# An encoder layer with mLSTM and attention: softmax sums over 64 rows, a second exp, dm in four steps, updates ahead of kw

## The chip, the cores and the metric

The kernel runs on one core of one Trainium2 chip. The core has a matrix engine (TensorE, "PE" in the profile, with its weight loads as "PEld"), a vector engine (VectorE, DVE), a scalar engine for activations (ScalarE, ACT), GpSimd (POOL) and SyncE (SP), which issues DMAs. Each engine executes its own instructions in the order in which they stand in its queue; semaphores make one wait for another. DMAs are issued from the queues of SP, ACT and POOL. The metric is the device time of one execution in microseconds (us), the median of several runs.

## What is computed

One encoder layer, run over 2048 prompt tokens and 256 sample tokens with the same weights, all in float32, width 1024:

```
h = rmsnorm(x, norm1_w)
mq, mk, mv, mo, gates, aq, ak, av = split(h @ w_in)
m_out = sigmoid(mo) * norm(mlstm_forward + mlstm_backward)     # 8 heads of 64
a_out = softmax(rope(aq) rope(ak)^T / 8) av                    # 8 query heads, 2 key heads of 64
x = x + concat(m_out, a_out) @ w_out
a, g = split(conv3(rmsnorm(x, norm2_w) @ w_up))
x = x + (silu(g) * a) @ w_down                                 # then a final rmsnorm
```

Attention is over the whole segment: queries of the prompt see the 2048 prompt tokens, queries of the sample the 256 sample tokens. mLSTM is a gated linear recurrence, computed in tiles of 128 tokens: inside a tile the products of queries and keys are multiplied by decay factors exp(dm), and between tiles a state C is carried on.

## The kernel before

Stages. `phase_a` (to about 250 us of the profile) computes the attention projections and the gates. Then `run_both` interleaves two generators, `attention` and `mlstm`, by costs that each yields, and when `mlstm` is done (about 1440 us) it calls on `phase_c`, the output projection, in its place. Attention ends at about 1840 us, `phase_c` at about 1915 us, and the rest is the feed-forward part, `phase_d`. Most float32 products are made of three fast matmuls of split operands: a value x is kept as a high part `hi` (a rounded copy) and a low part `lo = x - hi`, and x*y becomes hi*hi + hi*lo + lo*hi.

The program's order is not the final one. A scheduler takes the instructions as the code issues them, with priorities (`tc.high_priority`), and lays them out on each engine by a simulated time; after that the order on each engine is fixed, and only semaphores delay it. A tile of a pool with `bufs=n` can be written again when the one n before it has had its last reader.

Attention works on blocks of 512 queries (`hbs`): 32 large ones (4 query tiles of one head, 16 key tiles) and 4 small ones (2 key tiles). For block n:

- `prep` loads and transposes the queries, `maxstep` (L548) makes one 128x512 piece of scores `px` and its row maximum `mx` on DVE; a block needs 16, which are done during the steps of the block before.
- `scores(kp)` (L568) makes two key tiles' scores `ps` in PSUM, by two matmuls each (L575, L576), the second of which also subtracts the maximum. ACT exponentiates in place (L579) and copies to `ph` (L580), and DVE makes `pl = ps - ph` (L581). `px`, `ps` and other short-lived results share four PSUM banks (`SCB = 4`, tag "sc").
- `values(kp)` (L585) adds six matmuls into the single PSUM bank `pv` (L594), three for each key tile: vh*ph, vl*ph, vh*pl. `vh` has 66 columns: 64 of V and two of ones, so row 64 of `pv` is the sum of the probabilities. `values` runs `PLAG = 3` steps behind `scores`, with 8 buffers each of `ph` and `pl`; the last three steps of a block are done at its end.
- `fin1` (L596) copies 65 rows of `pv` to `o1` on ACT and sends row 64 to DRAM (`rs_d`), from where it is read back as `rc`, 128x4. `fin2`, in step 3 of the next block, takes the reciprocal on DVE (L609), writes it to DRAM and reads it back as `rb`, broadcast to 64 rows. `fin3`, in step 5, multiplies on POOL (L616) and writes the result to `mix_d`. `phase_c` reads `mix_d` as `cmx`.

mLSTM works on four pairs of heads. `proj_steps` (L891) goes through blocks of 256 tokens: `proj` (L714, L747 for the last pair) makes keys, queries, values and output gates; `projT` (L776) transposes the keys of the block before on PE into `mt`, copies them on ACT to `mkt` (L783, one buffer), and POOL multiplies them by weights into `kw` (L787, two buffers, one for each tile of 128); `upd` (L791) makes the state updates `mu` from `kw` (L800) and copies them to `C`, two steps behind `proj`. In one step `projT(b - 1)` is issued ahead of `upd(2b - 4)` and `upd(2b - 3)`.

`out_steps` (L907) makes a pair's outputs, tile by tile, beside the next pair's projections:

- `out_l` (L814) loads `dm`, 128x512, by a broadcast DMA from POOL's queue (L818), one tile ahead; `DMB = 4` buffers.
- `out_a` (L822) masks both directions on POOL (L825, affine_select), exponentiates the four parts on ACT (L828) and, for the first three pairs, loads the output gates `og` from POOL's queue (L833).
- `out_b`, one step on, multiplies `dm` by the scores `mS` on DVE (L844) and takes the part of the carried state, `mI`; `out_c`, two steps on, makes `mN` from `dm` and the values (L859) and divides by the denominator (L862 to L865); `rstd_of` makes `mr` on POOL; `out_n`, three steps on, applies it (L876); `out_d`, six steps on, transposes and writes to `mix_d`.

`proj_steps` and `out_steps` issue `projT`, `upd`, `out_b`, `out_c`, `out_n` and `out_d` at high priority.

Of the kernel before, what the change touches and what calls it, by code (L numbers as in the profile page):

```python
# [57 lines left out]
QZB = 2  # L58
RWM = 4
S1B = 2  # L60
DMB = 4
KWB = 2
CSTEP = 1
LEAD = 1.3
# [3 lines left out]
RW = 4  # L68
PO = 4
PB = 4  # L70
PHB = 8
PLB = 8
PLAG = 3
ZT = 3
SG = 3
RS = 2
# [384 lines left out]
def attention(g, tc, s1, s2, pp):  # L461
# [12 lines left out]
    def load_kv(grp, k0, k1, after=None):  # L474

        if (grp, k0) in kv:
            return
        n = k1 - k0
        sp = s2 if n == NT1 else s1
        kv[(grp, k0)] = parts = []  # L480
        for t0 in range(0, n, 4):
            m = min(4, n - t0)
            s = f"{n}_{t0}"
            kk = sp.tile([P, m * P], F32R, tag="kk" + s, name=f"kk{grp}_{s}", bufs=1)
            kl1 = sp.tile([65, m * P], F32R, tag="kl1" + s, name=f"kl1{grp}_{s}", bufs=1)
            vs = [sp.tile([P, m, HD + 2 * (1 - a)], F32R, tag=f"v{a}" + s, name=f"v{a}{grp}_{s}", bufs=1)
                  for a in range(2)]
            c = slice((k0 + t0) * P, (k0 + t0 + m) * P)
            if after is not None:
                for t in (kk[0:1, 0:1], kk[HD:HD + 1, 0:1], kl1[0:1, 0:1], vs[0][0:1, 0, 0:1], vs[1][0:1, 0, 0:1]):  # L490
                    nc.gpsimd.tensor_copy(t, after[0:1, 0:1])
            nc.gpsimd.memset(f32(vs[0][:, :, HD:]), 1.0)
            for r in (0, HD):
                nc.gpsimd.dma_start(f32(kk[r:r + HD, :]), g.k_d[grp, 0:HD, c])
            nc.gpsimd.dma_start(f32(kl1[0:HD, :]), g.k_d[grp, HD:P, c])
            nc.gpsimd.memset(f32(kl1[64:65, :]), 1.0)
            for a in range(2):
                nc.gpsimd.dma_start(f32(vs[a][:, :, 0:HD]), g.v_d[a, grp, :, k0 + t0:k0 + t0 + m])
            parts.append((kk, kl1, vs))
# [68 lines left out]
    def scores(s, kp):  # L568
        N = s.N
        parts = []  # L570
        for z in range(2):
            ps = pp.tile([P, 512], F32, tag="sc", name=f"ps{s.nm}_{kp}_{z}")[:, 0:N]
            kk, kl1, _ = s.kv[kp // 2]
            kc = (2 * kp + z) % 4 * P
            nc.tensor.matmul(ps, kk[:, kc:kc + P], s.qq[:, 0:N], start=True, stop=False)  # L575
            nc.tensor.matmul(ps, kl1[:, kc:kc + P], s.qm[:, 0:N], start=False, stop=True)  # L576
            ph, pl = (sp.tile([P, 512], F32R, tag=t, name=f"{t}{s.nm}_{kp}_{z}", bufs=n)[:, 0:N]
                      for t, n in (("ph", PHB), ("pl", PLB)))
            nc.scalar.activation(ps, ps, AF.Exp)  # L579
            nc.scalar.activation(ph, ps, AF.Copy)  # L580
            nc.vector.tensor_tensor(pl, ps, f32(ph), ALU.subtract)  # L581
            parts.append((ph, pl))
        return kp, parts

    def values(s, kp, parts):  # L585

        N = s.N
        if kp == 0:
            s.pv = pp.tile([P, 512], F32, tag="pv", name="pv" + s.nm, bufs=1)
        for z, (ph, pl) in enumerate(parts):  # L590
            kt = 2 * kp + z
            vh, vl = (v[:, kt % 4, :] for v in s.kv[kp // 2][2])
            for k, (v, p) in enumerate(((vh, ph), (vl, ph), (vh, pl))):
                nc.tensor.matmul(s.pv[0:HD if k == 1 else HD + 2, 0:N], v, p, start=(kt == 0 and k == 0), stop=(kt == s.nk - 1 and k == 2))  # L594

    def fin1(s):  # L596

        N = s.N
        s.o1 = sp.tile([HD + 1, 512], F32, tag="o1", name="o1" + s.nm, bufs=2)
        nc.scalar.activation(s.o1[:, 0:N], s.pv[0:HD + 1, 0:N], AF.Copy)  # L600
        s.n = len(done)
        done.append(s)
        nc.scalar.dma_start(g.rs_d[s.n:s.n + 1, 0], s.o1[HD:HD + 1, :])
        s.rc = sp.tile([P, 4], F32, tag="rc", name="rc" + s.nm, bufs=2)
        nc.sync.dma_start(s.rc, g.rs_d[s.n, 0].rearrange("(p k) -> p k", k=4))

    def fin2(s):

        nc.vector.reciprocal(s.rc, s.rc)  # L609
        nc.sync.dma_start(g.rs_d[s.n, 1].rearrange("(p k) -> p k", k=4), s.rc)  # L610
        s.rb = sp.tile([HD, 512], F32, tag="rb", name="rb" + s.nm, bufs=1)
        nc.sync.dma_start(s.rb, g.rs_d[s.n:s.n + 1, 1].to_broadcast([HD, 512]))

    def fin3(s):
        N = s.N
        nc.gpsimd.tensor_tensor(s.o1[0:HD, 0:N], s.o1[0:HD, 0:N], s.rb[:, 0:N], ALU.mult)  # L616
        for t0, (h, q0, q1) in part(s):
            r0 = HD * (h % 2)
            nc.gpsimd.dma_start(g.mix_d[q0 // 2:q1 // 2, r0:r0 + HD, 4 + h // 2].rearrange("n p t -> p n t"),
                                s.o1[0:HD, t0 * P:(t0 + q1 - q0) * P].rearrange("p (n t) -> p n t", t=BT))  # L620

    def fin4(s):

# [1 line left out]
            if h == 7:  # L625
                g.mixed.update(range(q0, q1))

    done = []
    cur = prep(0)
    while cur.todo:  # L630
        maxstep(cur)
# [4 lines left out]
    for n in range(len(hbs)):  # L636
# [3 lines left out]
        for kp in range(nkp):  # L640
# [11 lines left out]
                if not nxt.todo:  # L652
                    prep2(nxt)
            if old is not None:
                if kp == min(3, nkp - 1):
                    fin2(old)
                if kp == min(5, nkp - 1):
                    fin3(old)
# [10 lines left out]
                maxstep(nxt)  # L669
            prep2(nxt)  # L670
        old, cur = cur, nxt
    fin2(old)
    fin3(old)
    fin4(old)

# [1 line left out]
def mlstm(g, tc, s1, sp, sw, sn, pj_, pm):  # L677
# [141 lines left out]
                            g.nm_d[i, 4 * s.p:4 * s.p + 4].rearrange("r l -> (r l)").unsqueeze(0).to_broadcast([P, 4 * P]))  # L819
        return o  # L820

    def out_a(s, i, o):  # L822
        for d in range(2):
            sgn = 1 - 2 * d
            nc.gpsimd.affine_select(out=o.dm[:, d], in_=o.dm[:, d], compare_op=ALU.is_ge, fill=NEG, base=0,  # L825
                                    pattern=[[0, 2], [sgn, P]], channel_multiplier=-sgn)
            for h in range(2):
                nc.scalar.activation(o.dm[:, d, h], o.dm[:, d, h], AF.Exp,  # L828
                                     bias=tm[:, i, 0, d, 2 * s.p + h:2 * s.p + h + 1])
        if s.p < LASTP:  # L830
            if i % 2 == 0:
                s.og = s1.tile([P, 2, P], F32, tag="ogT", name=f"ogr{s.p}_{i}", bufs=OTB)
                nc.gpsimd.dma_start(s.og, g.og_d[s.p, i // 2])  # L833
            o.og = s.og[:, i % 2]

    def out_b(s, i, o):
        nm = f"{s.p}_{i}"
# [479 lines left out]
def body(tc, aps, phases="abcd"):  # L1317
# [5 lines left out]
    with ExitStack() as st:  # L1323
# [13 lines left out]
        dram("q_d", [NT, P, 8, P])  # L1337
        dram("k_d", [2, P, T])
        dram("v_d", [2, 2, P, NT, HD])
        dram("rs_d", [36, 2, 512])  # L1340
# [167 lines left out]
```

## Time and profile before

| What | us |
|---|---|
| median of 3 runs | 3524.24 (3521.58 to 3526.81) |
| the profiled execution's own time | 3521.41 |
| its span, first to last instruction | 3519.7 |
| window 0 to 250 (`phase_a`): PE busy | 215.02 |
| window 1840 to 1915 (end of `phase_c`): PE busy | 68.07 |
| window 1915 to 3520 (`phase_d`): PE busy | 1556.60 |

The profile's rows are read so. A group of instructions: line, engine, operation, what it writes and reads, shapes, count; then busy us in total and mean ns of one; then the idle time of the engine just before them and what ended most of it. A wait: who waited, for whom, us in total, times, the longest. A row of the timeline: start, duration, engine, line, operation, and in brackets the idle time of the engine before it with the instruction that ended it. Windows are in us from the start of the span. The matmuls of PE overlap, so the busy time of PE is that in which at least one was under way; the ends are modelled.

### The profile page before, as it was taken

To read this page: it belongs to the slowest core of one execution; us is meant where nothing else is said; L and a number is where in the kernel's file an instruction comes from. 1 tells how busy PE (TensorE), PEld (TensorE's weight loads), DVE (VectorE), ACT (ScalarE), POOL (GpSimd) and SP (SyncE) were. 2 spreads that over 40 slices of the span, in tenths; PEclk is the share of its full clock that TensorE was granted. 3 is DMA by queue.
4 is the path that set the end of the run, shared out by engine and by line. 5 is a ranking of instruction groups with operands and counts; after the bars stand their busy time and mean duration, and the time that the engine had idled before them with its cause. 6 is when DMAs were issued, how large, how long until landed. Compare 5 with 4: busy or idle time off the path is not lost. (4 is left out here: it accounts for less than half of the span.)

```text
span 3519.7 us, 56010 instructions
## 1 busy us (share of the span) xinstructions
PE 3362.7 (96%) x20058; PEld 3065.6 (87%) x20058; DVE 2562.9 (73%) x4546; ACT 1922.3 (55%) x4293; POOL 1109.7 (32%) x1312
## 2 busy tenths in 40 slices
PE   7989999999999999899989999999999999999998
PEld 6788887788888778687758999999999999999998
DVE  6874566566657676766654887878887879877777
ACT  4445656665666666545552544445544445655555
POOL 6653032223215322111115333224433224422222
PEclk9999999999999999999989999999999999999999
DMA  6765433243346445432228333213423223322221
GB/s 219 242 204 155 123 94 112 83 131 109 98 130 184 129 131 146 127 105 86 67 61 265 119 98 102 72 66 123 139 95 107 70 69 123 132 66 73 72 67 55
DMA packets 271310, 409.24 MB, mean 116 GB/s; under 512 B 44020, under 2 KB 168724, under 8 KB 271032
## 3 DMA queue, kind: packets, MB, share of 16 engines
q1 hardware_dynamic: 243312, 363.11, 32.4%
q0 software_dynamic: 11088, 33.04, 3.7%
q10 hardware_dynamic: 16632, 9.52, 0.9%
q8 instruction: 158, 2.59, 0.3%
q14 instruction: 120, 0.98, 0.1%
HBM read 321.52 MB, written 84.05 MB: 115 GB/s over the span
## 5 line engine op out<-in xcount | busy, mean ns | idle before, releaser
L1247 PE MATMUL pd<-act,wd 128*128 128x384 f32 (+1 forms) x3120 | 594.2, 337 | 23.1 <-DVE acc L1249 12.5
L1247 PEld LDWEIGHTS pd<-act,wd 128*128 128x128 f32 x3120 | 541.2, 189 | 30.6 <-DVE acc L1249 16.6
L581 DVE TENSOR_TENSOR pl<-ps,ph 128x512 fp32r<-128x512 f32 x520 | 351.3, 687 | 251.4 <-ACT ph L580 247.2
L1109 PE MATMUL pa<-nt,wut 128*128 128x386 f32 (+2 forms) x2376 | 453.7, 339 | 4.5 <-ACT u L1125 4.5
L1109 PEld LDWEIGHTS pa<-nt,wut 128*128 128x128 f32 x2376 | 420.6, 189 | 5.1 <-ACT u L1125 5.1
L553 DVE TENSOR_REDUCE mx<-px 128x1 f32<-128x512 f32 (+1 forms) x528 | 347.5, 676 | 69.7 <-PE px L552 67.2
L579 ACT ACTIVATE ps<-ps 128x512 f32<-128x512 f32 x520 | 297.5, 586 | 176.7 <-PE ps L576 165.8
L594 PE MATMUL pv<-ph,v 128*66 128x512 f32 (+1 forms) x1040 | 340.0, 404 | 24.6 <-ACT ph L580 24.1
L1203 DVE SCALAR_TENSOR_TENSOR y<-u,cw,y 128x768 f32<-128x768 f32 (+1 forms) x264 | 314.3, 1191 | 36.9 <-ACT y L1196 29.9
L1114 POOL TENSOR_TENSOR tw<-ru 128x512 f32<-128x512 f32 x66 | 93.4, 1416 | 739.7 <-DMA ru<-w_up 643.0
L1249 DVE TENSOR_TENSOR acc<-pd,acc 128x384 f32<-128x384 f32 (+1 forms) x544 | 281.2, 538 | 33.8 <-PE pd L1247 32.7
L1125 ACT ACTIVATE u<-pa 128x386 f32<-128x386 f32 (+2 forms) x264 | 128.4, 486 | 324.7 <-PE pa L1109 322.8
L580 ACT ACTIVATE ph<-ps 128x512 fp32r<-128x512 f32 x520 | 300.8, 597 | 7.8
L993 PEld LDWEIGHTS po<-cmx,wo 128*128 128x128 f32 x1728 | 231.5, 192 | 32.0 <-ACT cmx L979 11.3
L993 PE MATMUL po<-cmx,wo 128*128 128x256 f32 x1728 | 241.1, 284 | 12.2 <-ACT cmx L979 10.2
L575 PE MATMUL ps<-qq,kk 128*128 128x512 f32 x520 | 217.4, 421 | 2.9 <-ACT qm L566 1.7
L552 PE MATMUL px<-kk,qq 128*128 128x512 f32 (+1 forms) x528 | 212.8, 417 | 6.0 <-DVE mx L553 5.0
L594 PEld LDWEIGHTS pv<-ph,v 128*66 128x66 f32 (+1 forms) x1040 | 136.0, 138 | 85.8 <-ACT ph L580 35.1
L594 PE MATMUL pv<-pl,v 128*66 128x512 f32 x520 | 210.2, 404 | 0.3
L576 PE MATMUL ps<-qm,kl 65*128 65x512 f32 x520 | 207.6, 402 | 0.2 <-ACT qm L566 0.2
L721 PEld LDWEIGHTS mj<-mn,wm 128*128 128x128 f32 x1296 | 187.3, 196 | 23.2 <-DMA mn<-n_d 3.4
L721 PE MATMUL mj<-mn,wm 128*128 128x256 f32 x1296 | 201.2, 291 | 5.1 <-DMA mn<-n_d 3.2
(287 smaller groups left out, 7144.6 us busy)
## 6 DMA issues: line engine op xcount, KB each, us to landing
ru<-w_up SPq DMA_DIRECT2D x132, 512.0 KB
mn<-n_d SPq DMA_DIRECT2D x216, 256.0 KB
rd<-w_down SPq DMA_DIRECT2D x66, 512.0 KB
n_d<-n1T SPq DMA_DIRECT2D x18, 1024.0 KB
dm<-nm_d POOLq DMA_DIRECT2D x72, 256.0 KB, 3.9
mjn<-n_d SPq DMA_DIRECT2D x72, 256.0 KB
mvn<-n_d SPq DMA_DIRECT2D x72, 256.0 KB
q_d<-qz SPq DMA_DIRECT2D x18, 512.0 KB
```

What stands on the lines that cost most here:

```text
L553: nc.vector.tensor_reduce(s.mx[:, t, z0:z0 + 1], ps[:, 0:w], AX.X, ALU.max)
L575: nc.tensor.matmul(ps, kk[:, kc:kc + P], s.qq[:, 0:N], start=True, stop=False)
L579: nc.scalar.activation(ps, ps, AF.Exp)
L580: nc.scalar.activation(ph, ps, AF.Copy)
L581: nc.vector.tensor_tensor(pl, ps, f32(ph), ALU.subtract)
L594: nc.tensor.matmul(s.pv[0:HD if k == 1 else HD + 2, 0:N], v, p, start=(kt == 0 and k == 0), stop=(kt == s.nk - 1 and k == 2))
L721: nc.tensor.matmul(pj[:, o], s.w[c][:, a, o * P:(o + 1) * P], nT[c][:, :, h, :], start=(c + o + k == 0), stop=(c == NCC - 1 and k == 2 and ...
L993: nc.tensor.matmul(po[:, o], wo[c][z // 2][:, a, n], mx[c][:, h, :], start=(c == 0 and k == 0), stop=(c == NCC - 1 and k == 2))
L1109: nc.tensor.matmul(p, w[:, aa, c, :], ops[k][:, c, bb, 0:n], start=c == 0 and i == 0 and not add, stop=c == NCC // 2 - 1 and i == 2, skip_ ...
L1203: nc.vector.scalar_tensor_tensor(y[:, s:e], u[:, s + k:e + k], cw[:, k, jj:jj + 1], y[:, s:e], ALU.mult, ALU.add)
L1247: nc.tensor.matmul(po, wds[j][c // 4][:, aa, c % 4 * P:(c % 4 + 1) * P], acts[j][:, bb, z0:z1], start=(j == 0 and k == 0), stop=(j == len( ...
L1249: nc.vector.tensor_tensor(accs[c][:, z0:z1], po, accs[c][:, z0:z1], ALU.add)
```

## The change

- `ph` is written by a first exp from `ps`; a second exp then writes `ps` in place. The copy goes.
- The high part of V gets 128 columns, 64 of V and 64 of ones, so that rows 64 to 127 of `pv` each hold the sums. `values` does the four matmuls with `ph` first and then the two with `pl`. `PLAG` goes from 3 to 2, and `ph` and `pl` from 8 buffers to 6.
- `fin1` copies the 64 rows of sums to `rs` on ACT and no longer goes through DRAM; `fin2` takes the reciprocal of 64x128 in place, and is called four times, once in each of the first four steps of the next block (or four times in the last step of a short one); `fin3` multiplies by `rs`. Three DMAs a block and the tiles `rc`, `rb` and `rs_d` go.
- `out_a` is divided: `out_m` masks and loads the gates, `out_a` holds the exps and comes one step later; `out_b`, `out_c` and `out_n` come one step later too; `out_l` for the next tile is issued behind the mask. `dm` gets 6 buffers. `out_a` is now at high priority.
- In `proj_steps`, `upd` comes ahead of `projT`: `projT(b - 1)` goes behind the first yield.

```diff
-DMB = 4
+DMB = 6
-PHB = 8
-PLB = 8
-PLAG = 3
+PHB = 6
+PLB = 6
+PLAG = 2
...
-            vs = [sp.tile([P, m, HD + 2 * (1 - a)], F32R, tag=f"v{a}" + s, name=f"v{a}{grp}_{s}", bufs=1)
+            vs = [sp.tile([P, m, P if a == 0 else HD], F32R, tag=f"v{a}" + s, name=f"v{a}{grp}_{s}", bufs=1)
...
+            nc.scalar.activation(ph, ps, AF.Exp)
             nc.scalar.activation(ps, ps, AF.Exp)
-            nc.scalar.activation(ph, ps, AF.Copy)
             nc.vector.tensor_tensor(pl, ps, f32(ph), ALU.subtract)
...
-        for z, (ph, pl) in enumerate(parts):
-            kt = 2 * kp + z
-            vh, vl = (v[:, kt % 4, :] for v in s.kv[kp // 2][2])
-            for k, (v, p) in enumerate(((vh, ph), (vl, ph), (vh, pl))):
-                nc.tensor.matmul(s.pv[0:HD if k == 1 else HD + 2, 0:N], v, p, start=(kt == 0 and k == 0), stop=(kt == s.nk - 1 and k == 2))
+        vs = [[v[:, (2 * kp + z) % 4, :] for v in s.kv[kp // 2][2]] for z in range(2)]
+        todo = [(vs[z][k], parts[z][0]) for z in range(2) for k in range(2)] + [(vs[z][0], parts[z][1]) for z in range(2)]
+        for k, (v, p) in enumerate(todo):
+            nc.tensor.matmul(s.pv[0:HD if k in (1, 3) else P, 0:N], v, p, start=(kp == 0 and k == 0),
+                             stop=(2 * kp + 2 == s.nk and k == 5))
...
-        s.o1 = sp.tile([HD + 1, 512], F32, tag="o1", name="o1" + s.nm, bufs=2)
-        nc.scalar.activation(s.o1[:, 0:N], s.pv[0:HD + 1, 0:N], AF.Copy)
...
-        nc.scalar.dma_start(g.rs_d[s.n:s.n + 1, 0], s.o1[HD:HD + 1, :])
-        s.rc = sp.tile([P, 4], F32, tag="rc", name="rc" + s.nm, bufs=2)
-        nc.sync.dma_start(s.rc, g.rs_d[s.n, 0].rearrange("(p k) -> p k", k=4))
+        s.o1 = sp.tile([HD, 512], F32, tag="o1", name="o1" + s.nm, bufs=2)
+        s.rs = sp.tile([HD, 512], F32, tag="rs", name="rs" + s.nm, bufs=1)
+        nc.scalar.activation(s.o1[:, 0:N], s.pv[0:HD, 0:N], AF.Copy)
+        nc.scalar.activation(s.rs[:, 0:N], s.pv[HD:P, 0:N], AF.Copy)
+        s.left = list(range(0, N, P))
 
     def fin2(s):
 
-        nc.vector.reciprocal(s.rc, s.rc)
-        nc.sync.dma_start(g.rs_d[s.n, 1].rearrange("(p k) -> p k", k=4), s.rc)
-        s.rb = sp.tile([HD, 512], F32, tag="rb", name="rb" + s.nm, bufs=1)
-        nc.sync.dma_start(s.rb, g.rs_d[s.n:s.n + 1, 1].to_broadcast([HD, 512]))
+        if s.left:
+            r = s.rs[:, s.left[0]:s.left[0] + P]
+            s.left.pop(0)
+            nc.vector.reciprocal(r, r)
...
-                if kp == min(3, nkp - 1):
+                for _ in range(1 if kp < nkp - 1 else 4):
                     fin2(old)
...
-    def out_a(s, i, o):
+    def out_m(s, i, o):
+
         for d in range(2):
             sgn = 1 - 2 * d
             nc.gpsimd.affine_select(out=o.dm[:, d], in_=o.dm[:, d], compare_op=ALU.is_ge, fill=NEG, base=0,
                                     pattern=[[0, 2], [sgn, P]], channel_multiplier=-sgn)
-            for h in range(2):
-                nc.scalar.activation(o.dm[:, d, h], o.dm[:, d, h], AF.Exp,
-                                     bias=tm[:, i, 0, d, 2 * s.p + h:2 * s.p + h + 1])
...
+    def out_a(s, i, o):
+        for d in range(2):
+            for h in range(2):
+                nc.scalar.activation(o.dm[:, d, h], o.dm[:, d, h], AF.Exp,
+                                     bias=tm[:, i, 0, d, 2 * s.p + h:2 * s.p + h + 1])
...
-            if 1 <= b <= NB:
-                with tc.high_priority(offset=MPRI):
-                    projT(s, b - 1)
-            yield (6 if s.p < LASTP else 3) if b < NB else 0.5
             if 2 <= b:
                 with tc.high_priority(offset=MPRI):
                     upd(s, 2 * b - 4)
                     upd(s, 2 * b - 3)
+            yield (6 if s.p < LASTP else 3) if b < NB else 0.5
+            if 1 <= b <= NB:
+                with tc.high_priority(offset=MPRI):
+                    projT(s, b - 1)
             yield (6 if s.p < LASTP else 3) if b < NB else 0.5
...
-            if 2 <= i < NT + 2:
-                with tc.high_priority(offset=MPRI):
-                    out_c(s, i - 2, os_[i - 2])
-            if 1 <= i < NT + 1:
-                with tc.high_priority(offset=MPRI):
-                    out_b(s, i - 1, os_[i - 1])
-            if 3 <= i < NT + 3:
-                with tc.high_priority(offset=MPRI):
-                    out_n(s, i - 3, os_[i - 3])
-            for k in (i, i + 1) if i == 0 else (i + 1,):
-                if k < NT:
-                    os_[k] = out_l(s, k)
+            for lag, f in ((3, out_c), (2, out_b), (4, out_n), (1, out_a)):
+                if lag <= i < NT + lag:
+                    with tc.high_priority(offset=MPRI):
+                        f(s, i - lag, os_[i - lag])
+            if i == 0:
+                os_[i] = out_l(s, i)
             if i < NT:
-                out_a(s, i, os_[i])
+                out_m(s, i, os_[i])
+            if i + 1 < NT:
+                os_[i + 1] = out_l(s, i + 1)
```

More of the change, by code (lines that the diff above doesn't have):

```diff
@@ L589, in values @@
             s.pv = pp.tile([P, 512], F32, tag="pv", name="pv" + s.nm, bufs=1)
[L590 to L594 removed]
+        vs = [[v[:, (2 * kp + z) % 4, :] for v in s.kv[kp // 2][2]] for z in range(2)]
[3 more added lines that the diff above has]
+                             stop=(2 * kp + 2 == s.nk and k == 5))
     def fin1(s):
         N = s.N
[L599 to L605 removed]
+        s.o1 = sp.tile([HD, 512], F32, tag="o1", name="o1" + s.nm, bufs=2)
[3 more added lines that the diff above has]
+        s.left = list(range(0, N, P))
     def fin2(s):
[L609 to L612 removed]
+        if s.left:
+            r = s.rs[:, s.left[0]:s.left[0] + P]
+            s.left.pop(0)
+            nc.vector.reciprocal(r, r)
     def fin3(s):
         N = s.N
[L616 removed]
+        nc.gpsimd.tensor_tensor(s.o1[:, 0:N], s.o1[:, 0:N], s.rs[:, 0:N], ALU.mult)
         for t0, (h, q0, q1) in part(s):
@@ L619, in fin3 @@
             nc.gpsimd.dma_start(g.mix_d[q0 // 2:q1 // 2, r0:r0 + HD, 4 + h // 2].rearrange("n p t -> p n t"),
-                                s.o1[0:HD, t0 * P:(t0 + q1 - q0) * P].rearrange("p (n t) -> p n t", t=BT))
+                                s.o1[:, t0 * P:(t0 + q1 - q0) * P].rearrange("p (n t) -> p n t", t=BT))
     def fin4(s):
@@ L626, in fin4 @@
                 g.mixed.update(range(q0, q1))
-    done = []
     cur = prep(0)
@@ L671, in attention @@
         old, cur = cur, nxt
-    fin2(old)
+    for _ in range(4):
+        fin2(old)
     fin3(old)
@@ L1339, in body @@
         dram("v_d", [2, 2, P, NT, HD])
-        dram("rs_d", [36, 2, 512])
         dram("nm_d", [NT, 16, P])
```

## The prediction

> **What bounds the kernel now.** The page and the busy times by stage come first.
>
> ```profile
> span 3519.7 us, 56010 instructions
> PE 3362.7 (96%) x20058; PEld 3065.6 (87%) x20058; DVE 2562.9 (73%) x4546; ACT 1922.3 (55%) x4293; POOL 1109.7 (32%) x1312
> ...
> 250.00:1440.00 1190.00, 1141.87 (x7193) 962.51 (x7192) 763.38 (x1827) 735.66 (x2008) 326.98 (x680) 0.99 0.43 124
> 1440.00:1840.00 400.00, 381.15 (x2225) 304.20 (x2223) 258.47 (x468) 226.27 (x438) 51.37 (x49) 0.98 0.31 93
> ```
>
> After the window and its length the columns are PE, PEld, DVE, ACT, POOL busy, granted clock, DMA share, GB/s. The two windows are attention beside mLSTM, and attention beside the output projection; the edit touches nothing else but a short end behind them. PE is busy in 1141.87 of 1190 us and 381.15 of 400: it is the bound, and 48 + 19 = 67 us of idling are most of what can be won. What ends that idling is in the waits of PE's weight loads, for the first window and then the second, and behind them in those of ACT, POOL and DVE (first window; total, times, longest):
>
> ```profile
> PEld pv L594 <- ACT ph L580: 26.1, 20, 3.2
> PEld mN L859 <- ACT mkt L783: 6.2, 2, 5.1
> PEld ps L575 <- DVE pl L581: 5.8, 13, 0.5
> PEld px L552 <- DVE mx L553: 4.8, 12, 0.6
> ...
> PEld pv L594 <- ACT ph L580: 9.1, 13, 2.0
> PEld px L552 <- DVE mx L553: 9.0, 17, 2.6
> PEld ps L575 <- DVE pl L581: 4.4, 11, 0.5
> ...
> ACT dm L828 <- POOL dm L825: 155.5, 55, 10.9
> ...
> POOL dm L825 <- DMA dm<-nm_d: 186.4, 63, 4.8
> POOL kw L787 <- PE mu L800: 148.8, 35, 20.2
> POOL o L616 <- DMA rb<-rs_d: 133.6, 16, 26.3
> POOL dm L818 <- PE mN L859: 91.2, 21, 17.6
> ...
> DVE pl L581 <- ACT ph L580: 168.3, 143, 5.1
> DVE hh L876 <- POOL mr L98: 75.4, 43, 6.3
> ```
>
> The largest item is pv waiting for ph, 26.1 + 9.1 = 35.2 us in 33 waits. ph is late because ACT is: it executes in order and stood 155.5 us for the mask that POOL puts on dm. POOL in turn stood for kw, rb and dm's buffer. One such chain, from the timelines of POOL, ACT and PE:
>
> ```profile
> 547.78 1.19 POOL L787 TENSOR_TENSOR kw<-mkt,tm 128x256 f32<-128x256 f32 x2 [3.15 <-PE mu L800]
> 553.94 1.32 POOL L616 TENSOR_TENSOR o<-o,rb 64x512 f32<-64x512 f32 x1 [4.98 <-DMA rb<-rs_d]
> ...
> 556.21 0.59 POOL L818 DMA_DIRECT2D dm<-nm_d x1
> 560.17 0.77 POOL L825 TENSOR_SCALAR_AFFINE_SELECT dm<-dm 128x256 f32<-128x256 f32 x2 [3.36 <-DMA dm<-nm_d]
> 560.60 0.40 ACT L828 ACTIVATE dm<-dm,tm 128x128 f32<-128x128 f32 x1 [3.70 <-POOL dm L825]
> 560.91 0.58 ACT L580 ACTIVATE ph<-ps 128x512 fp32r<-128x512 f32 x1
> 561.54 0.68 PE L594 MATMUL pv<-ph,v 128*66 128x512 f32 x2 [1.12 <-ACT ph L580]
> ```
>
> POOL waits for rb until 553.94, issues the load of dm only at 556.21, masks at 560.17; ACT's exp of dm stands 3.70 us for it with a ph copy queued behind, and PE loses 1.12 us.
>
> **Two exps.** ACT's work stays the same, exp and copy taking as long:
>
> ```profile
> L580 ACT ACTIVATE ph<-ps 128x512 fp32r<-128x512 f32 x520 | 300.8, 597 | 7.8
> L579 ACT ACTIVATE ps<-ps 128x512 f32<-128x512 f32 x520 | 297.5, 586 | 176.7 <-PE ps L576 165.8
> ```
>
> An exp into SBUF is not in the trace; I take the copy's 597 ns. ph leaves ACT one operation sooner, 0.59 us. Over the 33 waits that is 19 us, as an upper figure, since some are shorter than 0.59. pl comes no sooner, and its matmuls now stand last in each group, behind four that need ph alone. **-19 us**.
>
> **Mask, buffers, kw, and no trip through DRAM.** The mask of a tile goes one step ahead of its exp, so ACT comes to a masked dm; six buffers let dm be loaded before the matmul two steps back has freed one (the 91.2 us row). The updates free the two kw buffers before kw asks for them (the 148.8 us row). fin3's product follows DVE instead of two DMAs (the 133.6 us row), and three DMAs a block leave the ACT and SP queues. Of the 35.2 us there remain 16 after the 19; I take two thirds, **-10 us**, since the other ACT waits are for PE's own scores. mN waiting for mkt is the kw chain (mkt's single buffer is held by kw): **-6 us**. The clock of 0.99 over 1190 us is 12 us lost to half-rate stretches behind idling; half of it, **-6 us**. At the end of attention
>
> ```profile
> 1843.34 0.59 ACT L600 ACTIVATE o<-pv 65x512 f32<-65x512 f32 x1 [7.13 <-DMA mix_d<-o]
> ...
> 1846.02 1.25 PE L993 MATMUL po<-cmx,wo 128*128 128x256 f32 x4 [7.42 <-ACT cmx L979]
> ```
>
> PE stands 7.42 us behind the rb trips of the last small blocks; **-4 us**. In all -45 us.
>
> Moving kw behind the updates has its own price: mt, mkt and kw now come half a projection step before the updates that use kw, not one and a half. If POOL is late, mu stands on PE with everything behind it; with POOL 27% busy (326.98 of 1190) I take **+1**, bound 0 to 0.63 us (kw's length, half of the 1.19 above) for each of 36 = 23.
>
> **The reciprocal** is the price. 36 of 128x4 go, 144 of 64x128 come. Rows near it (min/median/max ns):
>
> ```profile
> L864 DVE RECIPROCAL dn<-dn x72: 147/178/181, 445.0 to 1433.5; 128x4 f32<-128x4 f32 x72
> L862 DVE SCALAR_TENSOR_TENSOR dn<-s x72: 148/158/1177, 444.6 to 1432.8; 128x4 f32<-128x4 f32 x72
> L131 DVE TENSOR_SCALAR rcol_a<-rs_a x18: 143/150/159, 9.1 to 189.6; 128x1 f32<-128x1 f32 x18
> L876 DVE TENSOR_TENSOR hh<-hh,mr 128x128 f32<-128x128 f32 x72 | 21.9, 304 | 78.6 <-POOL mr L98 75.4 <-ACT ps L579 2.9
> ```
>
> At an element a step like L876 a piece costs 0.30 us, 44 in all. Were all of the 178 ns due to its 4 elements, 5.7 us and 820 in all. But it takes 20 ns more than L862 of equal size and 28 more than the TENSOR_SCALAR, 5 to 7 ns an element; with the 1.2 ns an element between L862 and L876 (146 ns over 124) that is 158 + 124 x 6.2 = 0.93 us to 150 + 124 x 8.2 = 1.17. I take their middle, 1.05 us: 151 us of DVE, less 6 for the old ones. DVE's share of the two windows goes from 1022 of 1590 us (64%) to 73%. The Trainium skill (VectorE: DVE Perf Modes, First, the fixed hardware budget) states that a reciprocal iterates its divide with a repeat count of 8; by its 0.96 GHz (Specifications) I estimate 1.07 us beside the fixed part, some 175 us for all. The excess in the rows points the same way as the page, not to the 0.30.
>
> This stretches DVE's queue, not PE's directly. PE's waits for DVE above are 5.8 + 4.8 + 9.0 + 4.4 = 24 us; each stands for one of four score banks. I let them nearly double, **+20 us**. What keeps it there: DVE itself stood 168.3 us for ph and 75.4 for POOL's mr, and both shrink with the stalls above. Bounds: 0, and the rival below.
>
> **Smaller costs.** Copying the sums takes 36 x 0.59 = 21 us of ACT, which has 454 us free in the first window; 0, at worst 21 as the single pv bank is held longer. The V weights grow from 66 to 128 columns in 1040 matmuls:
>
> ```profile
> L594 PEld LDWEIGHTS pv<-pl,v 128*66 128x66 f32 x520 | 72.5, 139 | 25.1 <-DVE pl L581 5.2 <-issue 0.4
> L552 PEld LDWEIGHTS px<-kk,qq 128*128 128x128 f32 x528 | 100.2, 192 | 28.9 <-DVE mx L553 13.8 <-DVE pl L581 2.7 <-issue 0.5
> ...
> 1526.54 0.39 PE L575 MATMUL ps<-qq,kk 128*128 128x512 f32 x1
> 1526.77 0.39 PE L576 MATMUL ps<-qm,kl 65*128 65x512 f32 x1
> 1527.00 0.39 PE L594 MATMUL pv<-pl,v 128*66 128x512 f32 x1
> ```
>
> A load of 128 columns takes 53 ns more, yet L576 behind it starts 0.23 us after its forerunner just as L594 behind 66 columns does: hidden, **+2**. The lag of values behind scores falls from three steps to two, so at a block's end 6 matmuls instead of 12 (0.23 us each) cover the last ph; scheduled fillers take part of it, 0 here, and a rival.
>
> **Sum.** -45 + 1 + 20 + 2 = -22 us. The profiled execution took 3521.4 us (its span and 1.7 around), so 3499.4; the median of the runs is 2.8 above it: **3502**.
>
> **Rivals.**
> 1. All the waits go. 35.2 + 6.2 + 7.4 of waits and the 12 of clock, less 9 of costs: -52, 3472. For it: one cause, ACT and POOL in order, is behind them all. Against: PE's waits for DVE cannot fall with more DVE work.
> 2. The short lag eats the gain. 1.38 us less cover a block, 0.59 regained by the early ph: 0.79 x 36 = 28 more, +6, 3530. For it: each block ends with scores whose ph is used at once. Against: 260 steps (the 520 copies of ph, two each) in 1590 us are 6.1 us each, so two still give 12 us in mid-block.
> 3. DVE becomes the bound, slower. The four pieces fall into a block's first four steps, where the next block's 16 maxima stand too. Two such halves:
>
> ```profile
> 646.90:673.00 26.10, 23.92 (x158) 20.60 (x158) 17.18 (x34) 12.80 (x38) 6.04 (x13) 1.00 0.32 99
> 1504.00:1529.00 25.00, 25.00 (x174) 22.32 (x173) 17.69 (x34) 9.50 (x19) 5.24 (x5) 1.00 0.46 133
> ```
>
> DVE is busy 17.18 and 17.69 us there, so 8.1 us on average are free, and 4.2 are to be added. It decides at 3.9 us: if more than that of DVE's in-order waiting stays, score banks come free late. If all stays, DVE is 4.2 us late; half reaching PE in 32 large blocks is 67 us in place of the 20: +25, 3549. Against it: the other half of a block is light, and the waits have a cause that goes.
> 4. The wide loads are on the path. The Trainium skill (TensorE: Matmul & The Clock Gate, LDWEIGHTS) lets a load's time grow with its columns. From the two rows, 53 ns x 1040 = 55 us would make 3555; the even 0.23 us speak against it.
>
> **How the numbers follow.** Forecast 0.46, rival 1 0.16, rival 2 with gains and costs cancelling 0.17, rival 3 0.18, rival 4 0.03. A measurement can tell about 0.2%, 7 us. Faster: the forecast and rival 1, 0.62; within it: 0.17; slower: 0.21. The range runs from rival 1 to just short of rivals 3 and 4: 3472 to 3545; the forecast's own is 3488 to 3516.
>
> **What would show it.** Right: ACT's wait for the mask under 50 us, POOL's kw and rb rows gone, pv's waits for ph under 15 us, PE busy over 97% in the first window. Reciprocals of about 1.05 us with PE's waits for mx and pl at 45 us confirm the price; at 0.3 us it is a term too large. Wrong: these waits above 70 us (rival 3), pv waiting as often as now (rival 2), or PE standing for kw.

## The result, and the profile after

The changed kernel takes 3479.4 us (median of 4 runs, 3475.2 to 3482.9), the one before 3522.9 (3517.7 to 3526.8). The ratio is 0.9877, with a 95% interval of 0.986 to 0.9894: some 43 us faster, about 37 to 49. The forecast was 3502, 22 us below the 3524 that was known of the kernel before.

First the page of the changed kernel, then its busy times by stage (columns as before: window, length, PE, PEld, DVE, ACT, POOL, clock, DMA, GB/s). Its stages end earlier, so the windows are cut at its own ends: mLSTM's last matmul at 1391, the last of attention at 1807, the first of the feed-forward part at 1874.

```profile
span 3476.8 us, 55736 instructions
## 1 busy us (share of the span) xinstructions
PE 3355.5 (97%) x20058; PEld 3109.2 (89%) x20058; DVE 2665.8 (77%) x4654; ACT 1928.2 (55%) x4329; POOL 1106.0 (32%) x1312
```

```profile
250.00:1391.00 1141.00, 1122.23 (x7170) 984.58 (x7169) 826.73 (x1890) 732.48 (x2021) 327.71 (x680) 0.99 0.43 127
1391.00:1807.00 416.00, 393.05 (x2246) 325.97 (x2246) 295.88 (x512) 234.69 (x461) 53.03 (x52) 0.96 0.28 87
1807.00:1874.00 67.00, 66.34 (x549) 65.82 (x549) 29.48 (x50) 16.41 (x30) 35.33 (x35) 0.98 0.79 252
1874.00:3476.80 1602.80, 1560.14 (x8916) 1549.09 (x8914) 1315.54 (x1822) 829.90 (x1645) 538.70 (x366) 0.99 0.29 95
```

And the end of the stage in the kernel before, the first row matching the third above:

```profile
1840.00:1914.80 74.80, 67.87 (x550) 67.41 (x551) 28.59 (x48) 16.96 (x31) 37.63 (x37) 0.92 0.74 237
1914.80:3519.70 1604.90, 1556.80 (x8914) 1546.13 (x8912) 1316.69 (x1822) 828.65 (x1644) 537.51 (x366) 0.99 0.29 94
```

The reader is to see three things. The first stage, attention beside mLSTM, is 49 us shorter (1190 to 1141), and PE idles 19 us of it in place of 48. The second is 16 us longer (400 to 416), with the clock at 0.96 in place of 0.98: this is where attention runs beside the output projection, and DVE is busy 71% of it in place of 65%. The end is 8 us shorter, at a clock of 0.98 in place of 0.92; the feed-forward part takes 2 us less, which is nothing.

The waits of PE's weight loads, for the first stage and then the second, and behind them those of ACT, POOL and DVE in the first:

```profile
PEld pv L593 <- ACT ph L579: 5.0, 10, 1.0
...
PEld px L552 <- DVE mx L553: 2.4, 6, 0.6
...
PEld pr L564 <- DVE m4r L561: 11.7, 5, 4.4
PEld px L552 <- DVE mx L553: 6.0, 9, 1.4
PEld pv L593 <- ACT ph L579: 4.8, 11, 1.0
PEld pv L593 <- DVE pl L581: 4.5, 8, 1.3
...
ACT dm L835 <- POOL dm L824: 109.8, 49, 9.4
...
POOL kw L785 <- ACT mkt L781: 181.4, 30, 22.0
POOL dm L824 <- DMA dm<-nm_d: 174.6, 62, 5.1
POOL dm L816 <- PE mN L861: 110.6, 27, 19.6
...
DVE pl L581 <- ACT ps L580: 134.5, 141, 4.8
DVE hh L878 <- POOL mr L98: 53.6, 34, 4.2
```

pv's waits for ph fell from 35.2 to 9.8 us, as foreseen. But POOL's did not fall: it stands longer for kw than before (181.4 against 148.8; it now waits for mkt, where it waited for mu), about as long for dm (174.6 against 186.4), longer for its buffer (110.6 against 91.2), and ACT still stands 109.8 us for the mask, where under 50 was foreseen. So what was to be the root of the gain is still there, while the gain is twice the forecast.

The reciprocal's own row, with the duration in ns as minimum, median and maximum:

```profile
L610 DVE RECIPROCAL rs<-rs x144: 883/886/946, 267.9 to 1811.5; 64x128 f32<-64x128 f32 x144
```

0.886 us a piece, 128 us in all; the forecast had 1.05 and 151.

### The profile page after: what moved, and what is told of

Its sections match the earlier page's. It is cut to its first block, busy times and chain, and to the rows that moved or that the text cites. A ratio compares the mean times of both kernels' runs of the same rounds, so it can differ in the third digit from the quotient of the medians.

```text
span 3476.8 us, 55736 instructions
## 1 busy us (share of the span) xinstructions
PE 3355.5 (97%) x20058; PEld 3109.2 (89%) x20058; DVE 2665.8 (77%) x4654; ACT 1928.2 (55%) x4329; POOL 1106.0 (32%) x1312
## 4 chain that ended last, share of the span: by engine, by line
PE 70%; DVE 11%; issue 6%; DMA 5%; ACT 4%; POOL 3%; SPq 0%; POOLq 0%; DVEq 0%; ACTq 0%
PE pa L1107 13%; PE pd L1245 12%; PE pv L593 8%; PE pc L1107 6%; PE po L991 5%; PE mj L719 4%; PE mv L729 3%; PE ps L575 3%; PE ps L576 3%; PE pb L1107 3%; PE px L552 2%; PE mv L745 1%; PE mN L861 1%; DVE y L1201 1%; DVE acc L1247 1%
## 5 line engine op out<-in xcount | busy, mean ns | idle before, releaser
L579 ACT ACTIVATE ph<-ps 128x512 fp32r<-128x512 f32 x520 | 309.8, 597 | 181.4 <-PE ps L576 177.0
L593 PE MATMUL pv<-ph,v 128*128 128x512 f32 (+1 forms) x1040 | 328.3, 405 | 4.0 <-ACT ph L579 2.1
L580 ACT ACTIVATE ps<-ps 128x512 f32<-128x512 f32 x520 | 310.8, 598 | 0.0
L576 PE MATMUL ps<-qm,kl 65*128 65x512 f32 x520 | 209.7, 406 | 0.0
L593 PE MATMUL pv<-pl,v 128*128 128x512 f32 x520 | 206.4, 408 | 1.7 <-DVE pl L581 1.5
L729 PE MATMUL mv<-wm,mn 128*128 128x256 f32 x1296 | 192.2, 286 | 2.3 <-ACT qb L725 2.0
```

The source lines that it names most:

```text
L593: nc.tensor.matmul(s.pv[0:HD if k in (1, 3) else P, 0:N], v, p, start=(kp == 0 and k == 0), stop=(2 * kp + 2 == s.nk and k == 5))
```

## The experiments

Ratios are to the kernel before, run on the same chip beside each; the us are the ratio's distance from 1 times 3523. The intervals are 3 to 10 us wide on either side, so that two kernels less than some 8 us apart are not told apart.

| Kernel | ratio (95% interval) | us |
|---|---|---|
| the change | 0.9877 (0.986 to 0.9894) | -43 |
| before, ratio of interleaving 1.31 (`b_lead`) | 0.9989 (0.9975 to 1.0002) | -4 |
| before + exps and order of values (`b_exps`) | 0.9882 (0.9861 to 0.9903) | -42 |
| before + exps (`b_expsonly`) | 0.9912 (0.9896 to 0.9927) | -31 |
| before + order of values (`b_vals`) | 0.9978 (0.9967 to 0.999) | -8 |
| before + dependent exps (`b_expdep`) | 0.9986 (0.9976 to 0.9995) | -5 |
| before + updates ahead of kw (`b_upd`) | 0.9998 (0.9983 to 1.0013) | -1 |
| before + lag of two (`b_lag2`) | 1.0006 (0.9994 to 1.0018) | +2 |
| change - exps and order of values (`a_noexps`) | 1.0005 (0.999 to 1.002) | +2 |
| change - sums in 64 rows (`a_nosums`) | 0.9955 (0.9937 to 0.9973) | -16 |
| change - dm steps and buffers (`a_nodm`) | 0.989 (0.9869 to 0.9911) | -39 |
| change - updates ahead (`a_noupd`) | 0.9886 (0.9863 to 0.9909) | -40 |
| change - reciprocals (`a_norecip`) | 0.9764 (0.9745 to 0.9782) | -83 |
| before + exps, order, lag (`b_exps_lag2`) | 0.9866 (0.985 to 0.9882) | -47 |
| the same + sums in 64 rows (`l_exps_sums`) | 0.9903 (0.9888 to 0.9918) | -34 |
| before + exps, order, lag + dm steps (`b_exps_lag2_dm`) | 0.9912 (0.989 to 0.9935) | -31 |
| change, sums in 128x256 (`a_half`) | 0.986 (0.9843 to 0.9878) | -49 |
| `a_half` - dm steps (`h_nodm`) | 0.979 (0.9763 to 0.9817) | -74 |
| `h_nodm` with a lag of three (`h_nodm_lag3`) | 0.9798 (0.9783 to 0.9812) | -71 |

### One part at a time on the kernel before

The edits are the lines of the diff that belong to the part; the control changes `LEAD` from 1.3 to 1.31.

```diff
-            nc.scalar.activation(ps, ps, AF.Exp)
-            nc.scalar.activation(ph, ps, AF.Copy)
+            nc.scalar.activation(ph, ps, AF.Exp)
+            nc.scalar.activation(ps, ps, AF.Exp)
```

> Kernel before with the two exps alone (and the order of values that goes with them: the four matmuls with ph, then the two with pl). Theory A (the gain is the early ph, as the prediction's first term has it): about -19 us, pv's waits for ACT's ph from 35 to about 16 us. Theory B (the gain comes from POOL's side, through masks, buffers and the sums; the exps only move the wait to pl): -5 us or less. Theory C (the scheduler draws a new order for any edit and the gain is mostly the luck of that draw): a difference of either sign that does not fit the waits.

> Kernel before with the updates ahead of kw alone. The prediction's terms: -6 us for mkt, a share of the -10 us of ACT's lateness, +1 for mu. Theory A: -3 to -8 us. Theory B: -10 us or more, with POOL's wait for kw gone. The profile of the changed kernel, where POOL still stands 181 us at kw (now for mkt), speaks for 0. Theory C: any sign.

> Kernel before with values two steps behind scores in place of three, and 6 buffers of ph and pl in place of 8. The prediction priced this at 0 and at +28 us in a rival. Theory A and B: 0 to +10 us. If the short lag costs, pv's waits for ph rise above 35 us.

> Control: kernel before with the interleaving ratio of the two generators at 1.31 in place of 1.30, so that the scheduler draws a slightly different order and nothing else changes. Theory A and B: within 7 us of before. Theory C: 10 us or more either way.

The exps with their order of values give 42 us, as much as the whole change. The updates give nothing, the lag costs nothing, and a new draw of the order by itself moves the time by 4 us, inside its interval. Theory A has the right part and half its size; pv's waits for ph fall to 12.5 us, where it foresaw 16. The other two parts, the sums in 64 rows and the dm steps, don't fit into SBUF beside 8 buffers each of `ph` and `pl`, and were tried only with 6.

### One part taken back from the changed kernel

The edits are the same lines the other way round.

> Changed kernel with exp and copy, and the old order of values, put back. Theory A (the early ph is the gain): about 20 us slower than the changed kernel, so some -24 us against before, with pv's waits for ph back at 20 us or more. Theory B (POOL's side is the gain): 5 us slower at most, -38 us against before.

> Changed kernel with the sums sent through DRAM again and V at 66 columns. The prediction has -4 us for the end, a share of the -10 us, and +20 us for the reciprocals in this part. If the +20 us is right, this kernel is 10 us or more faster than the changed one (-54 us against before). If the reciprocals cost nothing, it is 5 to 15 us slower (-30 to -38).

> Changed kernel with dm in three steps and four buffers again. Theory A: 5 us slower than the changed kernel. Theory B (masks and buffers are the gain): 15 us or more slower, with ACT's wait for the mask back at 150 us.

> Changed kernel with kw ahead of the updates again. Theory A: 6 us slower than the changed kernel. Theory B: 10 us or more slower. If mu waiting for a late kw costs more than the two kw buffers, it is faster instead.

Without the exps nothing is left of the gain: 45 us, agreeing with the 42. Dm steps and updates are worth 4 and 3 us, which can't be told from nothing; without the new dm steps ACT's wait for the mask is 84.7 us, not the 150 that theory B foresaw. The sums in 64 rows are worth 27 here, reciprocals and all: neither of the two cases foreseen. Together the four come to 79 us where the whole is 43, so the parts don't add.

### Why the two exps give 42 us and not 19

```diff
# b_expdep
-            nc.scalar.activation(ps, ps, AF.Exp)
-            nc.scalar.activation(ph, ps, AF.Copy)
+            nc.scalar.activation(ph, ps, AF.Exp)
+            nc.scalar.activation(ps, ps, AF.Exp, bias=f32(ph[:, 0:1]))
```

> Kernel before with the two exps alone, values in the old order (ph, ph, pl of one key tile, then of the other). Theory D (the copy stood not 0.59 us but some 1.3 us behind the exp, since it depends on it and the scheduler lays other work of ACT between; two exps depend on nothing and stand together): most of the 42 us, -30 to -42. Theory E (it takes the new order of values as well, since pl is no earlier by much): -15 us or less.

> Kernel before with the new order of values alone (four matmuls with ph, then two with pl), exp and copy as before. Theory D: within 7 us of before. Theory E: -10 us or more, as the second pair with ph then covers the wait for the first pl.

> Kernel before with two exps, of which the second takes the first column of ph as its bias, so that it depends on the first as the copy did; pl then holds other values than the reference needs. ph is early as with two free exps, pl and the score banks are as late as before. Values in the old order. If the early ph is the gain (the prediction's term, only larger): as much as two exps alone in the old order of values. If it is the early pl and the banks freed by it: half of that or less, with PE's waits for mx and pl as before.

31 us for the exps in the old order and 8 for the order make up the 42. The timelines of ACT show what the exps did. In the kernel before, the exp of the chain that the prediction quotes is at 555.52, its copy at 560.91:

```profile
555.52 0.59 ACT L579 ACTIVATE ps<-ps 128x512 f32<-128x512 f32 x1
556.32 0.26 ACT L871 ACTIVATE s<-hh 128x64 f32<-128x64 f32 x1 [0.20 <-DVE hh L868]
...
556.72 0.19 ACT L871 ACTIVATION_READ_ACCUMULATOR s<-hh 128x1 f32 x1
```

and in the changed kernel

```profile
557.51 0.60 ACT L579 ACTIVATE ph<-ps 128x512 fp32r<-128x512 f32 x1 [1.60 <-PE ps L576]
558.01 0.59 ACT L580 ACTIVATE ps<-ps 128x512 f32<-128x512 f32 x1
558.52 0.59 ACT L579 ACTIVATE ph<-ps 128x512 fp32r<-128x512 f32 x1
559.00 0.60 ACT L580 ACTIVATE ps<-ps 128x512 f32<-128x512 f32 x1
564.22 1.28 ACT L835 ACTIVATE dm<-dm,tm 128x128 f32<-128x128 f32 x4 [4.62 <-POOL dm L824]
```

A copy depends on its exp, and so other work of ACT comes between the two: here two squares and an exp of dm that waits 3.70 us for POOL's mask, with the copy queued behind. Of two exps of the same scores the second needs nothing that the first makes, and they stand together; ACT waits longer for the mask here (4.62 us), and both results of the scores are out before. Over all 520 pairs of each trace: L579 has L580 as the next ACT instruction in 304 cases before and 514 after. From the start of the second score matmul (L576), ph ends 3.19 us on in the mean before and 1.90 after; the last ACT result that pl needs ends 3.19 before and 2.39 after; pl ends 4.28 before and 3.56 after. So ph is 1.29 us earlier and not 0.59, and pl, of which the prediction said that it comes no sooner, is 0.72 earlier. With the two exps alone, `b_expsonly`, ph ends 1.91 and pl 3.52 on. pl's end gives a score bank back.

`b_expdep` parts the two. Its second exp depends on the first, and pl ends 4.24 us on, as before, while ph ends 1.86 on. It gives 5 us. PE's waits for ph, and for the maxima and pl that give banks back, over both stages of attention, in the kernel before, in `b_expsonly` and in `b_expdep`:

```profile
PEld pv L594 <- ACT ph L580: 35.1, 33, 3.2
PEld px L552 <- DVE mx L553: 13.8, 29, 2.6
PEld ps L575 <- DVE pl L581: 10.0, 23, 0.5
PEld pv L594 <- DVE pl L581: 5.2, 15, 0.5
PEld px L552 <- DVE pl L581: 2.7, 8, 0.5
```

```profile
PEld pv L594 <- ACT ph L579: 17.6, 12, 5.3
PEld px L552 <- DVE mx L553: 11.5, 14, 3.5
...
PEld px L552 <- DVE pl L581: 7.9, 10, 1.6
...
PEld ps L575 <- DVE pl L581: 6.1, 12, 1.2
...
PEld pv L594 <- DVE pl L581: 2.5, 5, 1.3
```

```profile
PEld px L552 <- DVE mx L553: 20.6, 31, 2.6
PEld ps L575 <- DVE pl L581: 15.8, 20, 2.7
PEld px L552 <- DVE pl L581: 13.0, 17, 1.6
...
PEld pv L594 <- DVE pl L581: 10.4, 15, 2.6
PEld pv L594 <- ACT ph L579: 9.6, 16, 2.3
```

With the dependent exps the waits for ph fall most, from 35.1 to 9.6 us, but PE stands for maxima and pl instead: the four rows sum to 59.8 us, where they had 31.7. With free exps they stay at 28.0, and ph's are down to 17.6. All waits of PE's weight loads that the view lists, from 250 us to the end of `phase_c`, sum to 136 us before, 128 in `b_expdep`, 98 in `b_expsonly` and 87 in `b_exps`; the 8, 38 and 49 us less go with the 5, 31 and 42 us of time. Of the 38 some 18 are ph's; the rest lies in many small rows, and why those fell is open. An early ph alone buys next to nothing. A reservation: the bias makes the second exp longer,

```profile
L580 ACT ACTIVATE ps<-ps,ph x520: 623/662/768, 262.3 to 1836.6; 128x512 f32<-128x512 f32 x174
```

662 ns where the changed kernel's takes 594, 35 us of ACT over 520. ACT has that time free, but part of the 26 us between this kernel and `b_expsonly` may be due to it. The Trainium skill (ScalarE: Activation LUTs, What ACT_TABLE_LOAD costs) has 93 ns for an operand of one column and the same for the overlap of two ACTIVATEs in a row; the 68 ns here are less, and two free exps overlap by some 120 ns (0.60 us less 0.48).

### The reciprocals

```diff
# a_norecip
-            nc.vector.reciprocal(r, r)
```

> Changed kernel without its 144 reciprocals: the outputs of attention are multiplied by the sums instead of divided. This takes 128 us of DVE out (144 of 0.886 us). If the prediction's +20 us for them is right: 15 us or more faster than the changed kernel, -58 us or more against before. If DVE hides them: within 7 us of the changed kernel, -37 to -50 against before.

40 us faster than the change, twice the term, in the one kernel that tells it. Its stages (mLSTM's end, attention's and the output projection's at 1431, 1767 and 1828):

```profile
250.00:1431.00 1181.00, 1163.82 (x7384) 1015.36 (x7383) 805.99 (x1865) 770.42 (x2095) 332.51 (x684) 1.00 0.41 123
1431.00:1767.00 336.00, 330.02 (x2034) 284.33 (x2035) 221.42 (x397) 195.04 (x387) 50.49 (x49) 0.99 0.34 106
1767.00:1828.00 61.00, 61.00 (x502) 60.85 (x501) 22.98 (x41) 15.12 (x26) 27.87 (x29) 0.97 0.74 236
```

PE idles 17 + 6 us in the first two stages, against 19 + 23 in the change: some 19 us. A like amount goes with the clock: 0.96 over 416 us of the change's second stage loses 17 us, 0.99 over 336 here 3, and the first stage has 1.00 over 1181 where the change has 0.99 over 1141. So the price is PE's idling and, by as much again, a lower clock, which the prediction left out of this term. That idling alone sets the clock is not shown: in `l_exps_sums` the second stage idles more than in the change, 25.87 us of 401, at a higher clock.

```profile
1406.00:1807.00 401.00, 375.13 (x2193) 310.98 (x2192) 283.35 (x498) 224.60 (x440) 53.94 (x53) 0.98 0.29 90
```

Of PE's waits the largest that goes is that of `pr` for the maxima, 11.7 us in the change's second stage; without the reciprocals it is, over both stages,

```profile
PEld pr L564 <- DVE m4r L561: 2.0, 3, 1.1
```

and the four rows for mx and pl sum to 11 us, where the change has 21.

### Lag, dm steps, updates and sums together

> Kernel before with the two exps, the new order of values, and the lag of two steps with 6 buffers. Without the lag this gave -42 us, with lag, dm and updates -16. Theory F (with sums through DRAM the short lag takes some 26 us back; a lag that cost nothing with a late ph costs once ph is early): -10 to -25 us. Theory G (dm and the updates take it back): -35 to -45 us.

> The same with the sums in 64 rows as well (so the changed kernel without the new dm steps, buffers and the moved updates). If the sums are worth their 27 us here too: -35 us or more, and dm and updates add the rest of the -43. If they are worth it only beside the new dm steps: no better than the kernel with exps and lag alone.

> Kernel before with two exps, the lag of two and the new dm steps with six buffers, updates behind kw as before, sums through DRAM. Exps and lag gave -47 us, dm and updates on top -16. If the dm steps take the 31 us back: -10 to -25. If the moved updates do: -40 or more.

With exps and lag alone the kernel is as fast as the whole change (-47 against -43). From there the sums in 64 rows cost 13 us, and the dm steps and updates on top of them give 9; without the sums, the dm steps cost 16, and the updates another 15 (`a_nosums`). Theory F on the lag falls. ACT's wait for the mask in the first stage goes with it: with exps and lag, with the dm steps added, with the updates added too, one trace each,

```profile
ACT dm L828 <- POOL dm L825: 107.0, 48, 5.9
```

```profile
ACT dm L837 <- POOL dm L826: 128.5, 51, 8.6
```

```profile
ACT dm L837 <- POOL dm L826: 153.3, 50, 8.8
```

It is 155.5 in the kernel before and 109.8 in the change. The step between mask and exp, which was to end this wait, raises it where the sums go through DRAM, and with the sums in 64 rows too (84.7 in `a_nodm`, 109.8 with the step). The edit also gives six buffers and puts `out_a` at high priority; the three weren't tried apart. Nor does this wait by itself tell the time: in `b_upd`, which is as slow as the kernel before, it is

```profile
ACT dm L828 <- POOL dm L825: 115.9, 54, 7.0
```

The updates don't free POOL either; in the last of the three above

```profile
POOL kw L787 <- ACT mkt L783: 137.2, 21, 19.4
POOL o L616 <- DMA rb<-rs_d: 133.2, 19, 27.5
```

kw comes to POOL's queue before mkt is made, and everything of POOL's stands behind it. Why the same edit gives a little in one surrounding and costs 15 us in another is left open: every edit makes the scheduler draw a new order. `b_lead` bounds only one such draw, at 4 us; the other edits of the kernel before that leave out the free exps (`b_upd`, `b_lag2`, `b_vals`, `b_expdep`) stay within 8, so a draw is unlikely to be the 31 to 45 us of the exps.

### A faster version

```diff
# a_half
-        nc.scalar.activation(s.o1[:, 0:N], s.pv[0:HD, 0:N], AF.Copy)
-        nc.scalar.activation(s.rs[:, 0:N], s.pv[HD:P, 0:N], AF.Copy)
-        s.left = list(range(0, N, P))
+        for z in range(2):
+            for t, r in ((s.o1, 0), (s.rs, HD)):
+                nc.scalar.activation(t[HD * z:HD * z + HD, :], s.pv[r:r + HD, 256 * z:256 * z + 256], AF.Copy)
+        s.left = list(range(0, 256, P))
```

> Changed kernel with o1 and the sums laid out as 128x256 (columns 256 to 511 in rows 64 to 127) by four ACT copies of 64x256, so that two reciprocals of 128x128 do the work of four of 64x128: 64 us of DVE less, POOL's product 128x256, one more DMA for each large block. If the price of the reciprocals is their time on DVE (40 us for 128): about 20 us faster than the changed kernel, -60 to -65 against before. If it is their place in the first steps of a block: half of that.

> The kernel with the 128x256 layout, values three steps behind with 7 buffers each, and dm in three steps with four buffers again (for the space). Theory F: faster than the 128x256 layout alone by 10 us or more. Theory G: within 7 us of it.

> The 128x256 layout with dm in three steps and four buffers, values two steps behind with 6 buffers. It stands between the layout with the new dm steps (-49 us) and that with the old dm steps and the lag of three (-71). If the longer lag made the 22 us: -40 to -55. If the old dm steps did, beside the layout: -60 or more.

The layout with half of the reciprocals' time gives 6 us beside the new dm steps, which can't be told from nothing and is far from the 20 foreseen, and 35 beside the old ones (`h_nodm` at -74 against `a_nodm` at -39). It also changes ACT's copies, POOL's product and the writes, so the gain is not DVE's time alone. The lag of three makes no difference here (-71 against -74), so the 22 us between `a_half` and `h_nodm_lag3` come with the old dm steps, and not with the lag as theory F had it; by what mechanism is not shown. `h_nodm` beats the change by some 31 us, and PE idles 14 us in each of its first two stages (1150 less 1136.60 and 380 less 365.29):

```profile
250.00:1400.00 1150.00, 1136.60 (x7264) 994.70 (x7263) 813.74 (x1865) 756.57 (x2100) 326.95 (x703) 1.00 0.43 126
1400.00:1780.00 380.00, 365.29 (x2164) 305.71 (x2163) 261.19 (x467) 220.44 (x453) 51.83 (x62) 0.98 0.31 95
```

## Why the prediction was right or wrong

The direction was right, and the time lies in the range; the size was half of what was measured, and the forecast's own range of 3488 to 3516 misses it. Of the signs that it named, pv's waits for ph (9.8 us) and PE's busy share of the first stage (1122.23 of 1141, 98%) came as written; ACT's wait for the mask, POOL's for kw and PE's for mx and pl did not. Term by term:

- **Two exps, -19.** The right part, too small: 42 us in the kernel before and 45 in the changed one. The step that failed is that the exps were priced by pv's waits for ph alone, with "ph leaves ACT one operation sooner, 0.59 us" and "pl comes no sooner". The copy stood behind whatever ACT did between exp and copy, masks included, so ph came 1.29 us sooner and pl 0.72. Pv's waits for ph fell by 17.5 us in `b_expsonly`, near the 19, though by another shift than the one assumed. But that fall alone is not the gain: `b_expdep` has more of it and stays within 5 us, since PE then stands for maxima and pl. What the free exps add over it is the early pl, and so the banks; with the reservation above that is what the runs show. The row quoted in the prediction had the exp of dm directly ahead of the copy, but not the exp that belongs to the copy, 5 us before.
- **The premise that PE's idling is most of what can be won.** It does not hold for the exps. Over the three stages from 250 us on, `b_exps` idles 18 us less than the kernel before, but PE's busy time is 24 us shorter as well (1590.89 to 1566.64), for nearly the same matmuls. Some 7 of the 24 go with the clock (0.983 to 0.986). A matmul of 512 columns lasts 0.39 us in the timeline and the next can start 0.23 us after it, so a shorter stall counts as busy; how much of the rest that is was not worked out.
- **Mask, buffers, kw, -22 without the end, and +1 for mu.** Not seen as single gains. The updates alone give 1 us; taking them or the dm steps back from the change costs 4 us at most. The waits of POOL for kw, dm and its buffer which were to go did not. PE's waits for mu that POOL ended come to 5.5 us in the change (3.7 and 1.8), against the +1. ACT's wait for the mask fell in the change (155.5 to 109.8), but 107.0 is reached without the new dm steps and updates, and 115.9 in `b_upd` at no gain in time.
- **The end, -4.** The end is 8 us shorter, and PE idles 0.7 us there in place of 6.9: the right mechanism, of which the term took only a part.
- **The reciprocal, +20.** Mis-sized: 40 in the one kernel that tells it. The duration was nearly right: 0.886 us against 1.05. The estimate that the prediction makes from the Trainium skill (VectorE: DVE Perf Modes, First, the fixed hardware budget) comes to 1.22 with its fixed part, and 0.30 by L876 was far off. What was wrong is the step from DVE's load to PE's waits. Those for mx and pl did not go to 45 us; they are 21 in the change and 11 without the reciprocals. `pr`'s wait for the maxima came in their place, and the lower clock, of which the term had nothing.
- **Copies, wide loads, lag, 0 to +2 each.** The lag of two gives +2 alone, within its interval, and -3 in `h_nodm` against `h_nodm_lag3`. The copies and loads weren't tried by themselves.

Rival 1 came nearest in time (3472) but not in reason, since POOL's and ACT's waits did not go. Rival 2, the short lag, is refuted. Rival 3 did not come about as a whole, but its mechanism is at work: the reciprocals cost twice the term, and most visibly in the second stage, where `pr` waits 11.7 us for the maxima. Rival 4 is not seen: a matmul of pv with 128 columns starts 0.23 us after the one ahead of it, in the median, as one with 66 did.

The sum came out too small by the exps' term. All the other parts together were forecast at -3 us, and the change without the exps is at +2 (`a_noexps`). That this came out near is luck, since the terms in it did not: 22 us of gains weren't seen, and the reciprocals cost 40 in place of 20. What made up for it is the sums in 64 rows, worth 27 us in the change with their reciprocals and so some 67 without them, where the prediction had some 14 at most (-10 and -4) for the trip through DRAM. But the same part costs 13 us beside exps and lag alone, so this is no fixed price, and why it differs is open.

## What to carry to other kernels

Where an engine makes two results from one input, let both start from the input: a second operation that depends on the first is not one operation late but as late as whatever is queued between them, and the buffer that it holds is late with it. A wait that PE shows is worth its length only if what PE waits for next is ready too; look for the scarce buffer (here four score banks) before pricing the wait. Test the parts of a bundle singly and by taking them back, since under a scheduler that redraws the order they don't add: here one part alone gave as much as the whole, and another, undone beside a new layout, gave 25 us more.

## What the runs showed of the hardware

- A reciprocal of 64x128 takes 886 ns and one of 128x4 178: 5.7 ns an element, where L876, a product of 128x128, takes 304 ns in all.
- Two ACT operations of 128x512 of which the second needs nothing that the first makes start 0.48 to 0.52 us apart though each lasts 0.60; a copy that depends on the exp directly before it starts 0.61 us after it (medians over the pairs).
- An exp of 128x512 from PSUM into SBUF takes the same as a copy: 597 ns each in the mean.
